# Splitting the last tile of a decoder trunk's output: 384 and 128 tokens in place of 256 and 256

## The chip, the cores and the metric

One core of a Trainium2 chip runs the whole program. The metric is the device time of one execution in microseconds; before the change it is 1289.63 us, the median of 3 runs (1287.84 to 1291.17).

## What is computed

A two-layer decoder trunk over 512 tokens of 1024 features in float32: a mixer (state-space and gated recurrence) and a gated ConvFFN, then dilated window attention and a second ConvFFN, and a final RMSNorm. The change touches only the very end, which the reference writes as

```python
    h = h + ff.astype(h.dtype)
return _rmsnorm(h, norm_final)
...
def _rmsnorm(x, g):
    xf = x.astype(jnp.float32)
    y = xf * lax.rsqrt(jnp.mean(xf * xf, axis=-1, keepdims=True) + NORM_EPS)
    return (y * g.astype(jnp.float32)).astype(x.dtype)
```

where `ff` is the down projection of the second ConvFFN: a product of 2816 by 1024 weights with the activations of 512 tokens.

## The kernel before

The activations are held transposed: a tile is 128 features (partitions) by 512 tokens (columns). The down projection in `ffn` (line 863) makes 8 such output tiles, `m` = 0 to 7, each a sum over `NF` = 22 blocks of the inner width. For full precision each block is three matmuls (`mm3`, lines 187 to 189): high weights by high activations, low weights by high activations, high weights by low activations, all in the reduced float32 format of TensorE (`F32R`), so 66 matmuls a tile. Each has weights of its own (128 by 128), which are loaded just ahead of it; its moving operand is the tokens.

In layer 1 the tiles `m` = 0 to 6 are made over all 512 tokens (lines 905 to 910), and as each is done, VectorE adds it to the residual `h` (line 909, tile H in the trace) and `norm_add` brings its squares into the sums `ss` and writes `hg`, which is h times the gain (tile xh in the trace; line 249 on ScalarE).

The last tile, `m` = 7, is made in two halves of 256 tokens (lines 914 to 926), so that the final norm of the first half's tokens runs beside the matmuls of the second half. For each half, in this order of dependence:

- 66 matmuls of 256 columns into a bank `pt`;
- line 921, VectorE: add to H;
- line 237, ScalarE: the square, into `sq`; line 249, ScalarE: `hg`;
- `rms_cols`, line 261, TensorE: small plain float32 matmuls with one column against a constant of 1/1024, first on `ss` (which is ready early), then on `sq`, so that the mean square of each token lands in a column of a bank `px`;
- lines 265, 207 and 210 to 212, VectorE: 11 tiny operations, the inverse root, into `rc`;
- `rms_rows`, line 273, TensorE: one transpose for each 128 tokens, which spreads `rc` over all partitions;
- line 925, VectorE: four products of two feature tiles each, `hg` times the inverse root, into `o` (tile xl in the trace);
- line 926: a DMA to the output after each product, by turns from the queues of SyncE (SP) and ScalarE (ACT).

Program order is not execution order: the framework's scheduler interleaves the instructions of one engine when the program is built, by its own estimates, and the order on each engine is then fixed. TensorE works strictly through that list of matmuls. So a small matmul of the first half's norm stands at a fixed place among the second half's matmuls, and TensorE waits there if its operand isn't ready.

Of the kernel before, what the change touches and what calls it, by code (L numbers as in the profile page):

```python
# [12 lines left out]
OP = mybir.AluOpType  # L13
# [3 lines left out]
KD = 8  # L17
# [138 lines left out]
class Kernel:  # L156
# [706 lines left out]
    def ffn(self, layer, gi):  # L863
        tc, nc, a, h = self.tc, self.nc, self.a, self.h
        V = nc.vector
        with tc.tile_pool(name="wkf", bufs=2) as self.wk, tc.tile_pool(name="ff1", bufs=1) as p1:
            self.nb = 5
            cw = p1.tile([128, 2 * NF, 4], F32, name="cw")
            nc.scalar.dma_start(cw, a["conv"][:, layer])
            ah = p1.tile([128, NF, T], F32R, name="ah")  # L870
            al = p1.tile([128, NF, T], F32R, name="al")
            hus = [p1.tile([128, T + 2], F32, name=f"hu{i}") for i in range(4)]
            for x in hus:
                nc.gpsimd.memset(x[:, 0:2], 0.0)
            w = Weights(self, a[f"w_f{layer}"], 1024)
            ahead = [self.proj(w) for _ in range(3)]
            rs = self.rms_rows(self.rms_cols())
            for j in range(NF):
                half = []
                for s in range(2):  # L880
                    f = 2 * j + s
                    x, pt, y = hus[f % 4], ahead.pop(0), self.tmp()
                    if f + 3 < 2 * NF:
                        ahead.append(self.proj(w))
                    V.tensor_tensor(x[:, 2:], pt, rs, op=OP.mult)  # L885
                    nc.scalar.activation(y, x[:, 2:], AF.Identity, scale=cw[:, f, 2:3], bias=cw[:, f, 3:4])  # L886
                    V.scalar_tensor_tensor(y, x[:, 1:T + 1], cw[:, f, 1:2], y, op0=OP.mult, op1=OP.add)  # L887
                    V.scalar_tensor_tensor(y, x[:, 0:T], cw[:, f, 0:1], y, op0=OP.mult, op1=OP.add)  # L888
                    half.append(y)
                nc.scalar.activation(half[0], half[0], AF.Silu)  # L890
                V.tensor_tensor(half[0], half[0], half[1], op=OP.mult)  # L891
                self.split(ah[:, j], al[:, j], half[0])
            w = Weights(self, a[f"w_g{layer}"], 1024)
            self.norm(gi, layer == 0)
            parts = []

            def block(m, q):
                n = m * NF + q
                if n // 8 == len(parts):
                    parts.append(w.next())  # L900
                hi, lo = parts[n // 8]
                b = slice(128 * (n % 8), 128 * (n % 8) + 128)
                return hi[:, b], lo[:, b]

            for m in range(KD if layer == 0 else KD - 1):
                pt = self.accbank()
                for q in range(NF):
                    self.mm3(pt, *block(m, q), ah[:, q], al[:, q], q == 0, q == NF - 1)
                V.tensor_tensor(h[:, m], h[:, m], pt, op=OP.add)  # L909
                self.norm_add(m, h[:, m])  # L910
            if layer == 0:
                return

            m = KD - 1
            o = self.xp.tile([128, KD, T], F32, name="xl")
            pts = [self.accbank() for _ in range(2)]
            for s in range(2):
                t = slice(256 * s, 256 * s + 256)
                for q in range(NF):
                    self.mm3(pts[s][:, t], *block(m, q), ah[:, q, t], al[:, q, t], q == 0, q == NF - 1)  # L920
                V.tensor_tensor(h[:, m, t], h[:, m, t], pts[s][:, t], op=OP.add)
                self.norm_add(m, h[:, m, t], t=t)
                rs = self.rms_rows(self.rms_cols(blocks=(2 * s, 2 * s + 1)), copy=False, blocks=(2 * s, 2 * s + 1))
                for i in range(0, KD, 2):
                    V.tensor_tensor(o[:, i:i + 2, t], self.hg[:, i:i + 2, t], rs[:, None, t].to_broadcast([128, 2, 256]), op=OP.mult)
                    (nc.scalar if i % 4 else nc.sync).dma_start(self.out[:, i:i + 2, t], o[:, i:i + 2, t])


    def attention(self):
# [335 lines left out]
```

## Time and profile before

| | |
|---|---|
| median of 3 runs | 1289.63 us (1287.84 to 1291.17) |
| the profiled execution's own time | 1289.94 us |
| its span, first to last instruction | 1288.1 us |
| TensorE busy | 1242.9 us, 96% of the span |
| VectorE busy | 812.5 us, 63% |
| ScalarE busy | 540.5 us, 42% |
| mean granted TensorE clock | 0.99 |

The span covers the instructions; the execution's own time is 1.84 us longer and holds what lies around them. Busy time is that of an engine's instructions, whether anything waits for them or not; what an engine is worth at a given place is read from the chain of waits and from the timeline there. In the timeline a row gives the start, the time taken, the engine and line, and the operands as out<-in; a matmul's time is that of one matmul from start to end, and since matmuls are pipelined, the step from one start to the next is the rate.

### The profile page before, as it was taken

How to read it: one execution, taken by the hardware profiler on the slowest of the kernel's cores; microseconds unless marked ns; L12 is line 12 of the kernel's file. 1: busy time of each engine (PE TensorE's matmuls, PEld its weight loads, DVE VectorE, ACT ScalarE, POOL GpSimd, SP SyncE). 2: the span in 40 equal slices, each digit the busy share in tenths (PEclk: the TensorE clock that was granted, in tenths of full speed). 3: DMA queues.
4: the chain of work that ended last, by engine and by line, in shares of the span. 5: the costliest groups of instructions: out<-in, count | busy, mean ns of one | idle time of the engine just before them, and what ended most of it. 6: DMA issues, size and time to landing. Idle time of an engine off the chain costs nothing.

```text
span 1288.1 us, 18925 instructions
## 1 busy us (share of the span) xinstructions
PE 1242.9 (96%) x7826; PEld 1019.4 (79%) x7826; DVE 812.5 (63%) x1342; ACT 540.5 (42%) x827; POOL 109.7 (9%) x87
## 2 busy tenths in 40 slices
PE   8889997999999999999999999999899999999997
PEld 6667775878888888888788887897688888888886
DVE  8786877958777776333563536556787777773223
ACT  6447646435444444222334333434354444442221
POOL 1443000110000000000120102100300000000000
PEclk9999998999999999999999999999999999999999
DMA  6532431232222222222322332322222222222211
GB/s 212 156 111 65 131 99 51 99 101 98 95 92 92 94 94 95 95 98 98 116 80 98 95 99 74 108 85 68 68 99 98 98 98 98 98 98 98 99 66 66
DMA packets 41126, 125.14 MB, mean 97 GB/s; under 512 B 18320, under 2 KB 22480, under 8 KB 28368
## 3 DMA queue, kind: packets, MB, share of 16 engines
q1 hardware_dynamic: 27744, 115.16, 27.2%
q10 hardware_dynamic: 13296, 8.78, 2.4%
q8 instruction: 61, 1.00, 0.3%
q14 instruction: 25, 0.20, 0.0%
HBM read 117.57 MB, written 4.78 MB: 95 GB/s over the span
## 4 chain that ended last, share of the span: by engine, by line
PE 83%; DVE 10%; DMA 2%; ACT 2%; issue 1%; POOL 1%; SPq 0%; DVEq 0%; ACTq 0%; POOLq 0%
PE pt L187 26%; PE pt L189 25%; PE pt L188 25%; DVE wlo L127 2%; PE px L1095 1%; DVE xl L231 1%; PE px L1120 1%; POOL g L765 1%; DMA b<-yd 1%; PE px L1179 1%; POOL g L758 1%; PE px L1092 0%; PE px L187 0%; PE px L847 0%; PE px L189 0%
## 5 line engine op out<-in xcount | busy, mean ns | idle before, releaser
L187 PE MATMUL pt<-xh,whi 128*128 128x512 f32 x1008 | 398.6, 396 | 4.0 <-ACT whi L126 2.3
L127 DVE TENSOR_TENSOR wlo<-stg,whi 128x1024 fp32r<-128x1024 f32 (+1 forms) x205 | 253.0, 1235 | 232.0 <-ACT whi L126 229.4
L189 PE MATMUL pt<-xl,whi 128*128 128x512 f32 x1008 | 393.8, 391 | 1.9 <-DVE xl L231 1.3
L188 PE MATMUL pt<-xh,wlo 128*128 128x512 f32 x1008 | 394.3, 391 | 0.3 <-DVE wlo L127 0.3
L126 ACT ACTIVATE whi<-stg 128x1024 fp32r<-128x1024 f32 (+1 forms) x205 | 214.3, 1046 | 264.4 <-PE pt L189 219.1
L187 PEld LDWEIGHTS pt<-xh,whi 128*128 128x128 f32 x1008 | 190.3, 189 | 46.3 <-issue 2.6
L189 PEld LDWEIGHTS pt<-xl,whi 128*128 128x128 f32 x1008 | 189.4, 188 | 43.1 <-DVE xl L231 2.4
L188 PEld LDWEIGHTS pt<-xh,wlo 128*128 128x128 f32 x1008 | 190.3, 189 | 39.8 <-DVE wlo L127 0.7
L187 PE MATMUL pt<-ah,whi 128*128 128x512 f32 (+1 forms) x374 | 142.4, 381 | 0.0
L189 PE MATMUL pt<-al,whi 128*128 128x512 f32 (+1 forms) x374 | 141.8, 379 | 0.0
L188 PE MATMUL pt<-ah,wlo 128*128 128x512 f32 (+1 forms) x374 | 140.4, 376 | 0.0
L885 DVE TENSOR_TENSOR hu<-pt,rs 128x512 f32<-128x512 f32 x88 | 60.2, 688 | 62.9 <-PE pt L189 60.0
L189 PEld LDWEIGHTS pt<-al,whi 128*128 128x128 f32 x374 | 70.2, 188 | 14.5
L188 PEld LDWEIGHTS pt<-ah,wlo 128*128 128x128 f32 x374 | 70.2, 188 | 13.9
L187 PEld LDWEIGHTS pt<-ah,whi 128*128 128x128 f32 x374 | 70.3, 188 | 12.4
L886 ACT ACTIVATE b<-hu,cw 128x512 f32<-128x512 f32 x88 | 70.7, 807 | 5.1 <-DVE hu L885 4.4
L193 ACT ACTIVATE ah<-b 128x512 fp32r<-128x512 f32 x44 | 27.7, 630 | 107.3 <-DVE b L891 107.3
L888 DVE SCALAR_TENSOR_TENSOR b<-hu,cw,b 128x512 f32<-128x512 f32 x88 | 65.9, 751 | 2.8
L887 DVE SCALAR_TENSOR_TENSOR b<-hu,cw,b 128x512 f32<-128x512 f32 x88 | 65.5, 746 | 0.0
L890 ACT ACTIVATE b<-b 128x512 f32<-128x512 f32 x44 | 27.8, 632 | 72.9 <-DVE b L888 72.9
L239 POOL TENSOR_TENSOR ss<-H 128x512 f32<-128x512 f32 x4 | 4.2, 1042 | 608.1 <-DVE H L909 506.7
L187 PE MATMUL pt<-whi,xh 128*128 128x512 f32 x128 | 53.5, 418 | 0.0
(308 smaller groups left out, 1438.4 us busy)
## 6 DMA issues: line engine op xcount, KB each, us to landing
stg<-w_f SPq DMA_DIRECT2D x44, 1024.0 KB
stg<-w_g SPq DMA_DIRECT2D x22, 1024.0 KB
stg<-w_qkv SPq DMA_DIRECT2D x18, 1024.0 KB
stg<-w_mix SPq DMA_DIRECT2D x8, 1024.0 KB
stg<-w_mo SPq DMA_DIRECT2D x4, 1024.0 KB
H<-xT SPq DMA_DIRECT2D x8, 256.0 KB
b<-xT ACTq DMA_DIRECT2D x8, 256.0 KB
wrow<-wd SPq DMA_DIRECT2D x8, 256.0 KB
```

The source lines that it names most:

```text
L126: nc.scalar.activation(hi[:, c], s[:, c], AF.Copy)
L127: nc.vector.tensor_tensor(lo[:, c], s[:, c], hi[:, c].bitcast(F32), op=OP.subtract)
L187: mm(pt, sh, mh, start=first, stop=False)
L188: mm(pt, sl, mh, start=False, stop=False)
L189: mm(pt, sh, ml, start=False, stop=last)
L193: nc.scalar.activation(hi, x, AF.Copy)
L231: nc.vector.scalar_tensor_tensor(self.xl[:, i], x, g, self.xh[:, i].bitcast(F32), op0=OP.mult, op1=OP.subtract)
L885: V.tensor_tensor(x[:, 2:], pt, rs, op=OP.mult)
L886: nc.scalar.activation(y, x[:, 2:], AF.Identity, scale=cw[:, f, 2:3], bias=cw[:, f, 3:4])
L887: V.scalar_tensor_tensor(y, x[:, 1:T + 1], cw[:, f, 1:2], y, op0=OP.mult, op1=OP.add)
L888: V.scalar_tensor_tensor(y, x[:, 0:T], cw[:, f, 0:1], y, op0=OP.mult, op1=OP.add)
L890: nc.scalar.activation(half[0], half[0], AF.Silu)
```

## The change

The last tile's two parts become blocks 0, 1, 2 (384 tokens) and block 3 (128 tokens). In the second part the products of line 925 take four feature tiles at a time in place of two, so that there are two of them and two DMAs.

```diff
-            for s in range(2):
-                t = slice(256 * s, 256 * s + 256)
+            for s, (blocks, n) in enumerate((((0, 1, 2), 2), ((3,), 4))):
+                t = slice(128 * blocks[0], 128 * blocks[-1] + 128)
                 for q in range(NF):
                     self.mm3(pts[s][:, t], *block(m, q), ah[:, q, t], al[:, q, t], q == 0, q == NF - 1)
                 V.tensor_tensor(h[:, m, t], h[:, m, t], pts[s][:, t], op=OP.add)
                 self.norm_add(m, h[:, m, t], t=t)
-                rs = self.rms_rows(self.rms_cols(blocks=(2 * s, 2 * s + 1)), copy=False, blocks=(2 * s, 2 * s + 1))
-                for i in range(0, KD, 2):
-                    V.tensor_tensor(o[:, i:i + 2, t], self.hg[:, i:i + 2, t], rs[:, None, t].to_broadcast([128, 2, 256]), op=OP.mult)
-                    (nc.scalar if i % 4 else nc.sync).dma_start(self.out[:, i:i + 2, t], o[:, i:i + 2, t])
+                rs = self.rms_rows(self.rms_cols(blocks=blocks), copy=False, blocks=blocks)
+                for i in range(0, KD, n):
+                    V.tensor_tensor(o[:, i:i + n, t], self.hg[:, i:i + n, t], rs[:, None, t].to_broadcast([128, n, 128 * len(blocks)]), op=OP.mult)
+                    (nc.scalar if i // n % 2 else nc.sync).dma_start(self.out[:, i:i + n, t], o[:, i:i + n, t])
```

On TensorE the change moves the small matmuls of the first part's norm to other places among the second part's matmuls. From the matmuls on `ss` to those on `sq` (both line 261; the last matmul of the first part stands just ahead of them), before:

```order
L261 MATMUL px<-cst,ss_9419 32x1 x8
L187 MATMUL pt<-ah,whi 128x256
L188 MATMUL pt<-ah,wlo 128x256
L189 MATMUL pt<-al,whi 128x256
L187 MATMUL pt<-ah,whi 128x256
L188 MATMUL pt<-ah,wlo 128x256
L189 MATMUL pt<-al,whi 128x256
L187 MATMUL pt<-ah,whi 128x256
L188 MATMUL pt<-ah,wlo 128x256
L261 MATMUL px<-cst,sq_10102 32x1 x8
```

and now:

```order
L261 MATMUL px<-cst,ss_9419 32x1 x12
L187 MATMUL pt<-ah,whi 128x128
L188 MATMUL pt<-ah,wlo 128x128
L189 MATMUL pt<-al,whi 128x128
L187 MATMUL pt<-ah,whi 128x128
L188 MATMUL pt<-ah,wlo 128x128
L261 MATMUL px<-cst,sq_10102 32x1 x12
```

So 8 of the second part's matmuls stood between the two and now 5 do, and each of the two has 12 small matmuls in place of 8. The second place is around the transposes of line 273, which wait for VectorE's `rc`; here with the tiles' numbers, of which 10006, 10045 and 10073 are the high weights of the tile's first 6, next 8 and last 8 blocks. Before:

```order
L188 MATMUL pt_10024<-ah_7741,wlo_10046 128x256
L189 MATMUL pt_10024<-al_7742,whi_10045 128x256
L187 MATMUL pt_10024<-ah_7741,whi_10045 128x256
L273 MATMUL px_10137<-cst_73,rc_10122 128x128 x2
L188 MATMUL pt_10024<-ah_7741,wlo_10046 128x256
L189 MATMUL pt_10024<-al_7742,whi_10045 128x256
```

and now:

```order
L189 MATMUL pt_10024<-al_7742,whi_10006 128x128
L187 MATMUL pt_10024<-ah_7741,whi_10006 128x128
L188 MATMUL pt_10024<-ah_7741,wlo_10007 128x128
L273 MATMUL px_10145<-cst_73,rc_10130 128x128 x3
L189 MATMUL pt_10024<-al_7742,whi_10006 128x128
L187 MATMUL pt_10024<-ah_7741,whi_10006 128x128
```

The transposes came in the ninth block and now come in the fifth: 17 matmuls stood between the `sq` matmuls and them, and now 9 do; 41 of the second part's 66 came behind them, and now 52 do.

On ScalarE the difference is this piece, from the last full tile's `hg` to the end of the program:

```order
 L249 ACTIVATE xh<-H,gn 128x512
-L237 ACTIVATE sq_10102<-H 128x256
-L249 ACTIVATE xh<-H,gn 128x256
-L926 DMA out<-xl 128x2x256 x2
-L237 ACTIVATE sq_10102<-H 128x256
-L249 ACTIVATE xh<-H,gn 128x256
-L926 DMA out<-xl 128x2x256 x2
+L237 ACTIVATE sq_10102<-H 128x384
+L249 ACTIVATE xh<-H,gn 128x384
+L926 DMA out<-xl 128x2x384 x2
+L237 ACTIVATE sq_10102<-H 128x128
+L249 ACTIVATE xh<-H,gn 128x128
```

Behind the last row stands one DMA of 128x4x128 in place of two. Nothing changes its place on ScalarE; the sizes do, and the second square still stands behind the first part's two DMAs. SP likewise issues two DMAs for the first part and one for the second in place of two, and VectorE two products in place of four at the end.

## Rows read from the trace of the kernel before

**Rows 1.** The page's head: the span.
```profile
span 1288.1 us, 18925 instructions
```

**Rows 2.** Busy time by stretch: us, PE, PEld, DVE, ACT, POOL, PEclk, DMA share, GB/s.
```profile
1268.69:1277.82 9.13, 9.08 (x101) 8.58 (x100) 4.68 (x16) 0.82 (x2) 0.00 (x0) 1.00 0.35 116
1277.82:1282.01 4.19, 1.08 (x35) 0.63 (x34) 2.20 (x13) 0.81 (x2) 0.00 (x0) 0.96 0.01 2
1282.01:1284.50 2.49, 0.00 (x0) 0.00 (x0) 2.48 (x4) 0.00 (x0) 0.00 (x0) 0.50 0.36 119
```

**Rows 3.** Timeline of TensorE: matmuls of the last full tile and the first half.
```profile
1254.42 0.39 PE L189 MATMUL pt<-al,whi 128*128 128x512 f32 x1
...
1260.60 0.39 PE L189 MATMUL pt<-al,whi 128*128 128x512 f32 x1
1260.83 0.28 PE L187 MATMUL pt<-ah,whi 128*128 128x256 f32 x1
...
1268.48 0.28 PE L189 MATMUL pt<-al,whi 128*128 128x256 f32 x1
```

**Rows 4.** Timeline during the second half: the first half's norm, and the last matmul.
```profile
1270.07 0.31 PE L261 MATMUL px<-cst,sq 128*32 128x1 f32 x16
...
1270.45 0.16 DVE L265 TENSOR_SCALAR ms<-px 128x2 f32<-128x2 f32 x1 [1.23 <-PE px L261]
...
1272.41 0.16 DVE L212 SCALAR_TENSOR_TENSOR rc<-rqt,rc 128x2 f32<-128x2 f32 x1
1272.63 0.43 PE L273 MATMUL px<-cst,rc 128*128 128x128 f32 x2
...
1273.02 0.28 PE L189 MATMUL pt<-al,whi 128*128 128x256 f32 x1
...
1273.10 2.48 DVE L925 TENSOR_TENSOR xl<-xh,px 128x512 f32<-128x512 f32 x4 [0.53 <-PE px L273]
...
1277.62 0.28 PE L189 MATMUL pt<-al,whi 128*128 128x256 f32 x1
```

**Rows 5.** The chain that ended last, behind the last matmul: start us, us, what.
```profile
1277.93 0.43 DVE H L921
...
1278.39 0.42 ACT sq L237
...
1278.86 0.35 PE px L261 x16
...
1281.50 0.48 PE px L273 x2
...
1282.01 0.69 DVE xl L925
```

**Rows 6.** Groups by line and shape: add and square of 512 columns (mean ns).
```profile
L909 DVE TENSOR_TENSOR H<-H,pt 128x512 f32<-128x512 f32 x15 | 10.3, 686 | 17.9 <-PE pt L189 17.9
L237 ACT ACTIVATE sq<-H 128x512 f32<-128x512 f32 x17 | 10.5, 618 | 3.9 <-DVE H L909 2.4 <-DVE ss L241 1.6
```

**Rows 7.** Plain float32 matmuls of 128 columns: timeline of layer 0, and their group.
```profile
123.77 0.60 PE L586 MATMUL px<-v,attd 128*128 128x128 f32 x4
...
126.00 1.04 PE L780 MATMUL px<-cst,g 128*128 128x128 f32 x8
```
```profile
L586 PE MATMUL px<-v,attd 128*128 128x128 f32 x32 | 5.5, 274 | 0.0
```

**Rows 8.** Weight loads by shape: 128 and 64 columns (busy us, mean ns).
```profile
L187 PEld LDWEIGHTS pt<-ah,whi 128*128 128x128 f32 x374 | 70.3, 188 | 12.4
...
L554 PEld LDWEIGHTS px<-hb 128*64 128x64 f32 x32 | 2.2, 138 | 2.5 <-DVE hb L570 1.8 <-issue 0.4 <-DVE hb L529 0.4
```

**Rows 9.** Output DMAs of the second half: issue, transfer; and packets of 512 bytes elsewhere.
```profile
1282.72 1.57 SPq L926 DMA_DIRECT2D out<-xl  x2
```
```profile
1283.40:1287.00 3.60, 0.00 (x0) 0.00 (x0) 1.09 (x2) 0.00 (x0) 0.00 (x0) 0.50 0.88 291
```
```profile
DMA packets 189, 0.09 MB, mean 269 GB/s; under 512 B 5, under 2 KB 189, under 8 KB 189
```

## The prediction

> **What bounds the kernel now.** The page's span [rows 1] is nearly all matmul stream, but the change lies in its last 28 us, so I read the stretches there first, then TensorE's timeline, and then the chain of waits behind the last matmul. TensorE is busy in 9.08 of the 9.13 us of the second half's stretch [rows 2], and the chain goes from its last matmul, which starts at 1277.62 [rows 4], through VectorE's add, ScalarE's square, the small matmuls, the transposes and the products [rows 5] to the output DMAs. Two things thus set the end: how long the second part's matmuls run, and how long the tail behind them is. The change shortens the tail and cannot take a column off the stream: 384 + 128 is 256 + 256.
>
> From the rates to see in the timeline [rows 3]: 27 steps from 1254.42 to 1260.60 give 0.2289 us a matmul of 512 columns; 65 steps from 1260.83 to 1268.48 give 0.1177 us at 256. The difference is 0.1112 us for 256 columns, so 384 columns should take 0.1733 us. This lies between two measured sizes and is safe. For 128 columns the trace has no matmul of this format at all, and on that price the forecast turns.
>
> **The price at 128 columns.** Carrying the line of the two sizes on gives 0.0621 us, the low end. But every matmul has 128 columns of weights of its own to load. A load of 64 columns is 138 ns and one of 128 is 188 ns [rows 8], 0.78 ns a column, so 128 columns keep the load path for 0.10 us if loads don't overlap each other. At 256 columns that is hidden under the columns themselves; at 128 it is not. The nearest rows with this tile shape are layer 0's plain float32 matmuls of 128 columns with 128 columns of weights: from 123.77 to 126.00 there are 20 of them (4, 2, 2, 4, 2 and 6 in a row), 0.1115 us each [rows 7]. They read their columns differently, so they don't prove the load bound, but they show that loads can follow each other at that pace, and they agree with the 0.10. I take **0.1115 us**: barely less than at 256 columns. The high end is 0.2289 us, if 128 columns cost what 512 do now; the rows for it are under the first rival.
>
> The Trainium skill (TensorE: Matmul & The Clock Gate, section Back-to-back issue gap) gives about 81 ns a matmul as the sustained rate of load and matmul pairs at 128 columns, less than rows 7 show; by it the sum below would be 50 x 0.0305 = 1.5 us lower, an estimate from that page. No row here goes as low for a full load, so I don't take it.
>
> **The stream, step by step.** The first part starts where it did, 1260.83, and its last matmul starts at 1260.83 + 65 x 0.1733 = 1272.09. The first part's norm then follows the pattern of the second half's tail:
> - Matmul start to add: 0.31 us (1277.62 to 1277.93), and 0.05 more for a longer matmul: 1272.46.
> - Add to square: 0.46 us at 256 columns; 512 columns take 0.686 in place of 0.43 [rows 6], so 384 add 0.13: 1273.05.
> - Square to the `sq` matmuls: 0.47 us; 618 ns in place of 0.42 at 512 columns, so 384 add 0.10: 1273.62.
> - `sq` matmuls to the mean: 0.38 us (1270.07 to 1270.45), and half of 0.35 us again for half as many more: 1274.17.
> - Mean to transposes: 2.18 us (1270.45 to 1272.63 [rows 4]), whatever the number of columns, 2 or 3: 1276.35.
>
> In the new order only nine matmuls stand between the `sq` matmuls and the transposes. At 0.1115 they take 1.0 us, and the norm takes 2.7. So **a new wait** opens: TensorE stands still for about 1.2 us ahead of the transposes, with the other 52 matmuls queued behind. Before, 17 matmuls of 0.1177 filled nearly that time. From the transposes to the second matmul behind them it was 0.39 us (1272.63 to 1273.02); one more transpose adds 0.11 (the eight of line 780 take 1.04 us [rows 7]): 1276.85. The last matmul starts 50 steps later: 1276.85 + 50 x 0.1115 = 1282.43, against 1277.62: **+4.8 us**.
>
> **The tail.** With 128 columns in place of 256 the last matmul ends 0.05 us sooner; the add saves 0.13 and the square 0.10 (the same slopes as above); half of the small matmuls go, 0.17 of 0.35; one transpose of two goes, 0.11. Together -0.56. The 11 tiny operations between keep their time: they have two elements a partition or one. So the first product starts at 1282.01 + 4.8 - 0.56 = 1286.26.
>
> From its start the old tail took 4.99 us until the last data had left (1282.01 to 1287.00): the first DMA is issued at 1282.72, data flow from about 0.8 us later, and the queue is full from then on, 1.05 MB at 291 GB/s over 3.6 us [rows 9]. Now the first product is as long as before (512 elements), data flow from 1.5 us after its start, and half of the bytes remain. They go in runs of 512 bytes in place of 1024; the trace has a stretch of such packets at 269 GB/s, so 0.52 MB take 1.95 us: 3.45 in place of 4.99, **-1.5 us**. If a packet of 512 took the time of one of 1024 nothing would be won there; if the rate held at 291, another 0.15. The second of the two products ends at 1.3 us and its DMA's data can flow from 2.1 us, within that time.
>
> Costed at nothing: the first part's products, 4 of 768 elements in place of 512, take 2.48 x 1.5 = 3.7 us [rows 4] and end near 1280.7, before the second part's add at 1282.7; and ScalarE, whose second square stands behind two DMAs that wait for these products, is free by then. The work that hides both is the second part's stream; it is cover only while that stream lasts.
>
> **Sum:** 4.8 - 0.56 - 1.5 = +2.7 us. The profiled execution took 1289.94 us, its span 1288.1; it lies 0.3 above the median of the three runs. 1289.63 + 2.7 = **1292.3 us**, 0.21% more. About 0.3%, 3.9 us, is what a measurement of this kernel can tell from no change, so I call this the same.
>
> **Rivals.**
>
> *First, a matmul of 128 columns is far dearer than one of 256.* Line 586 is called 16 times in the program (four heads, four blocks) and has 32 records [rows 7]: a plain float32 product of 128 columns takes two passes of 0.1115, so 0.22 us, what 512 columns of the reduced format cost. If TensorE handles the reduced format like plain float32 in short matmuls, or streams it in one quarter of the speed, the price is 0.22 to 0.2289. Against it: from 512 to 256 columns nothing but a fixed 0.0065 us stays [rows 3]. The transposes would come at nearly the same time, since five and nine matmuls then take 1.15 and 2.1 us, about what the norm takes. The end moves by 50 x (0.2289 - 0.1115) = 5.9, 0.17 for a longer last matmul and some 0.1 of shift: 2.7 + 6.1 = +8.8, **1298.4 us**, slower. It decides from 0.135 us a matmul on, where 2.7 + 50 x 0.0235 passes 3.9. The Trainium skill (FP8 and Floating Point Precision, section TensorE Precision Notes) keeps four passes for true float32 and has the reduced format read and cut down, without a word on length; that speaks against the rival, and no row here shows it at 128 columns.
>
> *Second, columns alone count.* At 0.0621 the stream ends 2.5 us sooner, but the first part's products then hold VectorE until 1280.7, where the add would be due at 1280.2: +2.7 - 2.5 + 0.4 = +0.6, **1290.2 us**. For it: the straight line from 512 to 256. Against it: rows 7 and 8. Even so there is no gain, as the new wait eats it.
>
> *Third, the granted clock falls in the new wait.* It is 1.00 through the second half, 0.96 over the 4.2 us behind it, which hold few matmuls, and 0.50 after that [rows 2]. At 0.50, the lower of its two levels, 1.2 in place of 2.4 GHz, the 52 matmuls would take 0.22 us each and the time would be near that of the first rival, 1298. Against it: the wait is 1.2 us, and in the tail the clock held for some 3.5 us behind the last big matmul.
>
> **How the numbers follow.** Forecast 0.55, first rival 0.34, second 0.06, third 0.03, and 0.02 for a gain that I don't see. The forecast's own range is 1290.8 (price 0.10, cheap data) to 1294.0 (price 0.1177, dear packets, the scatter of the runs); a tenth of it lies above 3.9 us and counts as slower. Faster by over 0.3%: 0.02. Within: 0.5 and the second rival, 0.55. Slower: 0.34, 0.03 and 0.06, so 0.43. Cases of two kinds hold the chance, so the range takes both: 1289.9 to 1299.4.
>
> **What would show it.** Steps of 0.173 us in the first part; a step of 0.11 in the second (0.06 or 0.22 for the rivals); TensorE waiting about 1.2 us for `rc` ahead of the transposes of line 273 (none if the price is 0.22); the last matmul near 1282.4; 4.5 us from the first product of the last tail to the end of the span, against 6.1. If the granted clock drops between 1274 and 1282, the third rival is right. If the end of the stream lies before 1280, my price is wrong on the low side.

## The result, and the profile after

The change makes the kernel slower. Its median is 1296.33 us (1295.50 to 1298.94, 6 runs) against 1290.00 (1287.84 to 1291.17, 6 runs of the kernel before, the three known ahead of the prediction among them); the ratio is 1.0055, with a 95% interval of 1.0042 to 1.0069, so +7.1 us (5.4 to 8.9). The time lies in the predicted range, but not where the likeliest case put it: 1292.3, no difference that can be measured. What happened is the third rival, which had 0.03. That the range holds the time is luck: it reached that far for the first rival's price, which the rows below exclude.

The page's head of the kernel after answers to [rows 1]; the execution that was profiled took 1295.50 us, with a mean granted clock of 0.984 against 0.99:

```profile
span 1293.7 us, 18920 instructions
```

Spans of two executions can't simply be subtracted here: the last tile's first part starts at 1260.83 in [rows 3] and at 1257.71 now, and over all the profiles of this study at 1257.15 to 1260.83, with nothing changed in the code ahead of it. So I count from that start, called S below. From S to the end of the span it was 27.27 us before, and it is 35.99 now: +8.7.

Windows by stage of the kernel after, with the columns of [rows 2] (stretch and its length, then busy time of PE, PEld, DVE, ACT and POOL, PEclk, DMA share, GB/s). The stretches are the first part's matmuls; from there to the last matmul ahead of the new wait; the wait, cut in two where the clock fell; the matmuls behind it; the tail; the output:

```profile
1257.71:1269.10 11.39, 11.39 (x67) 11.28 (x65) 2.52 (x3) 0.96 (x2) 2.33 (x2) 1.00 0.00 0
...
1269.31:1272.10 2.79, 2.52 (x63) 2.21 (x62) 1.47 (x7) 1.03 (x2) 0.00 (x0) 1.00 0.02 6
1272.10:1272.54 0.44, 0.00 (x0) 0.00 (x0) 0.37 (x3) 0.00 (x0) 0.00 (x0) 1.00 0.00 0
1272.54:1273.20 0.66, 0.00 (x0) 0.00 (x1) 0.50 (x4) 0.00 (x0) 0.00 (x0) 0.50 0.00 0
...
1273.20:1284.67 11.47, 11.47 (x54) 11.47 (x55) 3.55 (x4) 0.00 (x0) 0.00 (x0) 0.50 0.38 137
1284.67:1288.89 4.22, 1.37 (x19) 0.81 (x19) 2.04 (x12) 0.60 (x2) 0.00 (x0) 0.50 0.00 0
1288.89:1293.70 4.81, 0.00 (x0) 0.00 (x0) 1.28 (x2) 0.00 (x0) 0.00 (x0) 0.50 0.39 109
```

Read the PEclk column downwards. It is 1.00 (2.4 GHz) until 0.44 us into the wait, then 0.50 (1.2 GHz), and it never comes back, although TensorE is busy in all 11.47 us of the stretch behind. In [rows 2] the second half ran at 1.00 from start to end.

The timeline of the kernel after, answering to [rows 3, 4] (in the gaps the pattern repeats):

```profile
1268.97 0.34 PE L189 MATMUL pt<-al,whi 128*128 128x384 f32 x1
...
1269.35 0.56 DVE L921 TENSOR_TENSOR H<-H,pt 128x384 f32<-128x384 f32 x1 [6.27 <-PE pt L189]
...
1270.57 0.37 PE L261 MATMUL px<-cst,sq 128*32 128x1 f32 x24 [0.26 <-ACT sq L237]
...
1271.04 0.28 PE L187 MATMUL pt<-ah,whi 128*128 128x128 f32 x1
...
1271.82 0.28 PE L188 MATMUL pt<-ah,wlo 128*128 128x128 f32 x1
...
1272.98 0.16 DVE L212 SCALAR_TENSOR_TENSOR rc<-rqt,rc 128x3 f32<-128x3 f32 x1
...
1273.20 0.90 PE L273 MATMUL px<-cst,rc 128*128 128x128 f32 x3 [1.11 <-DVE rc L212]
...
1274.22 0.41 PE L188 MATMUL pt<-ah,wlo 128*128 128x128 f32 x1
...
1284.67 0.41 PE L189 MATMUL pt<-al,whi 128*128 128x128 f32 x1
```

The 384-column step is (1268.97 - 1257.71) / 65 = 0.1732 us. The 128-column step ahead of the wait is (1271.82 - 1271.04) / 7 = 0.111. Then TensorE stands still for 1.11 us, for `rc`. Behind it the same matmuls step by (1284.67 - 1274.22) / 49 = 0.2133 us: from 0.111 to 0.213, nearly twice, with the clock at half.

The chain that ended last, behind the last matmul, answering to [rows 5]:

```profile
1285.12 0.30 DVE H L921
1285.44 0.32 ACT sq L237
1285.81 0.33 PE px L261 x8
1288.41 0.46 PE px L273
1288.89 0.69 DVE xl L925
```

From the last matmul to the first product it is 4.22 us (4.39 before), and from there to the end of the span 4.81 (6.09 before). The sum of the changes: the last matmul at S + 26.96 against S + 16.79, +10.17; -0.17 and -1.28 behind it; +8.7.

### The profile page after: what moved, and what is told of

Same layout as the page of the kernel before. It is cut to its first block, busy times and chain, and to the rows that moved or that the text cites. A ratio compares the mean times of both kernels' runs of the same rounds, so it can differ in the third digit from the quotient of the medians.

```text
span 1293.7 us, 18920 instructions
## 1 busy us (share of the span) xinstructions
PE 1249.8 (97%) x7826; PEld 1026.5 (79%) x7826; DVE 814.1 (63%) x1340; ACT 540.5 (42%) x827; POOL 109.7 (8%) x87
## 4 chain that ended last, share of the span: by engine, by line
PE 83%; DVE 10%; DMA 2%; issue 2%; ACT 1%; POOL 1%; DVEq 0%; ACTq 0%; SPq 0%; POOLq 0%
PE pt L187 26%; PE pt L189 26%; PE pt L188 25%; DVE wlo L127 2%; PE px L1095 1%; DVE xl L231 1%; PE px L1120 1%; PE px L1179 1%; POOL g L765 1%; POOL g L758 1%; PE px L1092 0%; DVE hb L570 0%; DVE ss L241 0%; PE px L847 0%; PE px L546 0%
## 5 line engine op out<-in xcount | busy, mean ns | idle before, releaser
L187 PE MATMUL pt<-ah,whi 128*128 128x512 f32 (+2 forms) x374 | 146.0, 390 | 0.0
L189 PE MATMUL pt<-al,whi 128*128 128x512 f32 (+2 forms) x374 | 145.4, 389 | 0.0
L188 PE MATMUL pt<-ah,wlo 128*128 128x512 f32 (+2 forms) x374 | 143.9, 385 | 0.0
L189 PEld LDWEIGHTS pt<-al,whi 128*128 128x128 f32 x374 | 72.9, 195 | 14.5
```

The lines of the kernel that those rows point to most:

```text
L187: mm(pt, sh, mh, start=first, stop=False)
L188: mm(pt, sl, mh, start=False, stop=False)
L189: mm(pt, sh, ml, start=False, stop=last)
```

## The experiments

Two theories stood at the start, and the third came up after the first four runs. **A**: the standstill ahead of the transposes lets the clock fall. **B**: the matmuls of 128 columns ("narrow" below, those of 256 "wide"), which the prediction takes to go at the pace of their weight loads, make it fall by themselves. **C**: the narrow matmuls ahead of the wait have a share in it too. For all but one of the experiments the last tile was written so that its order on TensorE can be set: `k1` and `k2` are the numbers of the second part's matmuls ahead of the small `sq` matmuls (the sums) and ahead of the transposes, 5 and 14 in the change, `cols` the columns that the second part's matmuls run over. Where `force` is set, each piece is tied behind the small matmuls on TensorE's list:

```diff
-            for s, (blocks, n) in enumerate((((0, 1, 2), 2), ((3,), 4))):
...
+            first, second, cols, k1, k2, force = ((0, 1, 2), 2), ((3,), 4), slice(384, 512), 5, 14, True
...
+            late(0, k1)
+            rc = self.rms_cols(blocks=first[0])
+            with after(self.last):
+                late(k1, k2)
+            rs = self.rms_rows(rc, copy=False, blocks=first[0])
+            with after(self.last):
+                late(k2, 3 * NF)
```

The diffs below are against this form. Where `cols` is wider than 128 columns, the columns outside block 3 go to a part of the bank that nothing reads. Every ratio below is against runs of the kernel before on the same chip. The experiments were spread over three chips, so where two of them are compared it is by these ratios or by their spans from S, which are those of one profile each.

**No wait.** The sums and transposes come so late that neither waits.

```diff
-            first, second, cols, k1, k2, force = ((0, 1, 2), 2), ((3,), 4), slice(384, 512), 5, 14, True
+            first, second, cols, k1, k2, force = ((0, 1, 2), 2), ((3,), 4), slice(384, 512), 17, 46, False
```

> Parts of 384 and 128 tokens as in the change, but the first part's sums stand behind 17 of the second part's matmuls and its transposes behind 46, so that nothing makes TensorE wait inside the second part. Theory A (the 1.3 us wait ahead of the transposes drops the granted clock, and it stays down because nothing raises it again): no wait, so the clock stays 1.00 through the second part, all its steps are 0.111 us, and the kernel is about 1.2 us over the kernel before (+3.2 us of matmuls, -2.0 us of tail). Theory B (the load-paced matmuls of 128 columns drop the clock by themselves): the clock falls to 0.50 about 3 us into the second part although there is no wait, the steps behind that are 0.21 us, and the kernel is 4.5 to 6.5 us over.

Measured: 1291.23 us (1287.97 to 1293.72, 10 runs), ratio 1.0023 (1.0009 to 1.0038). The second part's matmuls, in the windows of this kernel:

```profile
1270.67:1278.90 8.23, 8.23 (x124) 8.07 (x123) 4.48 (x15) 1.03 (x2) 0.00 (x0) 1.00 0.04 12
```

The clock holds over all 66 narrow matmuls; the last one starts at S + 19.59, not 26.96. That speaks for A and against B. But the transposes are late now, and the cover that the prediction named for the first part's products is gone. From the timeline of VectorE (here line 934 is the products, line 949 the second part's add):

```profile
1276.75 3.55 DVE L934 TENSOR_TENSOR xl<-xh,px 128x768 f32<-128x768 f32 x4 [1.58 <-PE px L273]
1280.22 0.28 DVE L949 TENSOR_TENSOR H<-H,pt 128x128 f32<-128x128 f32 x1
```

The add could have started 0.32 us behind the last matmul of 1278.62, at 1278.94, and waits 1.28 us for the products. Theory A had the whole at 1.2 us over the kernel before, without this wait; from S to the end it is 2.7 us over.

**The old halves, with the change's wait.** Parts of 256 and 256, sums behind 5 and transposes behind 14.

```diff
-            first, second, cols, k1, k2, force = ((0, 1, 2), 2), ((3,), 4), slice(384, 512), 5, 14, True
+            first, second, cols, k1, k2, force = ((0, 1), 2), ((2, 3), 2), slice(256, 512), 5, 14, True
```

> Halves of 256 and 256 as before the change, but with the wait of the change: the first half's sums behind 5 and its transposes behind 14 of the second half's matmuls, and the other 52 held behind them. Theory A: the clock falls in the wait of about 1.2 us as it does with the change, and the 52 matmuls of 256 columns then take 0.21 us or more for as long as it stays down: 5 to 7 us over the kernel before. Theory B: the clock stays 1.00, the steps stay 0.118 us, and only the waits are paid: about 1.5 us over.

Measured: 1289.92 us (one run). The clock falls, from the timeline's steps just behind the wait, and it comes back:

```profile
1269.62:1273.36 3.74, 3.74 (x19) 3.74 (x20) 2.48 (x4) 0.00 (x0) 0.00 (x0) 0.54 0.45 146
1273.36:1277.70 4.34, 4.34 (x42) 4.20 (x44) 0.00 (x0) 0.00 (x0) 0.00 (x0) 1.00 0.34 116
```

So a wait among matmuls of 256 columns can cost the clock too, but there it is back after some 3.4 us. Neither theory had that: from S the end is 2.7 us later than before, where A had 5 to 7 us, with the clock down for longer, and B about 1.5, without a fall.

**The change's wait with 256 columns behind and ahead.** The second part's matmuls run over 256 columns, and half of that is thrown away.

```diff
-            first, second, cols, k1, k2, force = ((0, 1, 2), 2), ((3,), 4), slice(384, 512), 5, 14, True
+            first, second, cols, k1, k2, force = ((0, 1, 2), 2), ((3,), 4), slice(256, 512), 5, 14, True
```

> The change with its wait (sums behind 5, transposes behind 14 matmuls of the second part), but the second part's matmuls run over the last 256 tokens, of which the first 128 are thrown away: the same number of matmuls and loads, twice the columns. Theory A: the clock falls in the wait as with the change; the steps behind it are 0.21 us or more, and the kernel is 7 us or more over the kernel before. Theory B: the clock stays 1.00 and the steps 0.118 us, twice the columns are faster than half of them, and the kernel is about 3 us over (+3.6 first part, +1.5 waits, -2.0 tail).

Measured: 1290.58 us (one run), with the clock at 1.00 through the wait and behind it:

```profile
1272.66:1273.76 1.10, 0.10 (x2) 0.00 (x1) 0.87 (x6) 0.00 (x0) 0.00 (x0) 1.00 0.00 0
1273.76:1280.20 6.44, 6.44 (x62) 6.31 (x63) 3.55 (x4) 0.00 (x0) 0.00 (x0) 1.00 0.63 224
```

Twice the columns, and from S to the end 30.53 us where the change takes 35.99: the columns are not what the change pays for. By itself this run came out as B expected (clock 1.00, about 3 us over; from S 3.3 us); it is the first sign that the standstill alone doesn't settle the matter: as long a wait, and no fall.

**The narrow part first.** Block 0, then blocks 1 to 3.

```diff
-            for s, (blocks, n) in enumerate((((0, 1, 2), 2), ((3,), 4))):
+            for s, (blocks, n) in enumerate((((0,), 4), ((1, 2, 3), 2))):
```

> The 128 tokens first and the 384 second: 66 matmuls of 128 columns follow the 512-column stream with nothing between them. Theory A: clock 1.00 and 0.111 us a step throughout, 7.3 us for the first part; the kernel is about 5.5 us over the kernel before, for the longer tail of 384 tokens. Theory B: the clock falls to 0.50 some 3 us into the first part, the rest of it runs at 0.21 us a step, so the part takes 10 us or more; whether the 384-column matmuls behind it raise the clock again shows what keeps it down.

Measured: 1293.35 us (one run). The 66 narrow matmuls run in 7.4 us at full clock:

```profile
1259.03:1266.40 7.37, 7.37 (x67) 7.33 (x65) 2.51 (x3) 0.96 (x2) 2.31 (x2) 1.00 0.00 0
```

With the first experiment this ends theory B: where no standstill stood among them or ahead of them, the narrow matmuls ran at full clock to the last. From S the end is 5.2 us later than before (A had about 5.5): 3.0 of it at the last matmul, and 2.2 behind it, where the tail now has 384 tokens.

**The wait filled.** The change's order, and five matmuls of 512 columns between the 14th matmul and the transposes, whose result is not used.

```diff
-                late(k1, k2)
+                self.mid = late(k1, k2)
+            with after(self.mid):
+                fb = self.auxbank()
+                for i in range(5):
+                    hi, lo = block(m, 0)
+                    self.fil = nc.tensor.matmul(fb, hi, ah[:, 0], start=True, stop=True)
+            with after(self.fil):
                 rs = self.rms_rows(rc, copy=False, blocks=first[0])
```

> The change with its order (sums behind 5, transposes behind 14 matmuls of the second part), but five matmuls of 512 columns into a bank that nobody reads fill the wait ahead of the transposes. Theory A (the standstill drops the clock): the clock stays 1.00 through the second part, steps of 0.111 us, and the kernel is 2.5 to 3 us over the kernel before, what the sum without a clock change gave. Theory B (the light matmuls drop it, or the light matmuls and small sums around the wait): the clock falls as with the change, 52 steps of 0.21 us, 6 to 8 us over.

Measured: 1292.81 us (1291.65 to 1293.71, 5 runs), ratio 1.0037 (1.0024 to 1.0050). The wait's stretch, and the matmuls behind it:

```profile
1274.77:1276.14 1.37, 1.37 (x8) 0.84 (x7) 1.02 (x7) 0.00 (x0) 0.00 (x0) 1.00 0.00 0
1276.14:1282.40 6.26, 6.26 (x61) 6.19 (x63) 3.55 (x4) 0.00 (x0) 0.00 (x0) 1.00 0.62 222
```

TensorE does work that nothing needs, the transposes come 0.1 us later than with the change (S + 15.59), and the last matmul starts 5.4 us sooner, at S + 21.58. That is +4.79 against before, where the prediction had +4.8 for a clock that holds. Theory A had 2.5 to 3 us over for the whole; from S to the end it is 3.2, while the ratio makes it 4.8 (3.1 to 6.5).

**Wide ahead of the wait, narrow behind.** Here `cols` is set for each of the second part's matmuls, by its number `i`.

```diff
+                    cols = slice(256 if i < 14 else 384, 512)
```

> The same order and the wait left empty; the second part's first 14 matmuls run over 256 columns (128 thrown away), the 52 behind the wait over 128. Theory A in the form that the standstill alone decides: the clock falls in most runs and stays down for the 52, so 6 to 8 us over the kernel before. Theory C (the 14 light matmuls ahead of the wait count too, since the same wait behind wide ones kept its clock in one look and lost it for 3.4 us in another): in a good part of the runs the clock holds and they are about 3 us over, in the others it falls, and with 128 columns it doesn't come back.

Measured: 1290.81 us (1289.33 to 1297.50, 10 runs), ratio 1.0026 (1.0012 to 1.0040). Eight of the ten lie at 1289.3 to 1293.0 and two at 1295.4 and 1297.5; the profile is of one of the two. The wait, and the stretches to the fall and behind it:

```profile
1274.15:1275.15 1.00, 0.00 (x1) 0.00 (x0) 0.81 (x5) 0.00 (x0) 0.00 (x0) 1.00 0.00 0
1275.15:1277.42 2.27, 2.27 (x21) 2.27 (x21) 1.69 (x2) 0.00 (x0) 0.00 (x0) 1.00 0.00 0
1277.42:1285.40 7.98, 7.80 (x45) 7.59 (x43) 2.15 (x4) 0.04 (x1) 0.00 (x0) 0.50 0.55 197
```

The clock falls not in the wait but 2.3 us behind it, in the middle of narrow matmuls that follow each other without a gap, and then stays down. By their times eight of the ten runs are of the kind that C had (about 3 us over, which is also the median) and not of A's (6 to 8 us over in most).

**Narrow ahead, wide behind.**

```diff
+                    cols = slice(256 if i == 0 or i >= 14 else 384, 512)
```

> The mirror image: 13 of the first 14 matmuls over 128 columns, then the empty wait, then 52 matmuls over 256 columns (128 thrown away). The clock should fall in the wait as with the change in all theories but one that blames the light matmuls behind it; what is tested is the way back: if full columns raise it as in the halves with a wait (back after 3.4 us), about 14 of the 52 run at 0.23 us and the rest at 0.118, so the kernel is 4 to 5 us over the kernel before, faster than the change though it streams twice the columns; if the clock stays down to the end as with the change, it is 8 us over or more.

Measured: 1293.12 us (1290.41 to 1295.70, 7 runs), ratio 1.0034 (1.0019 to 1.0049), in two groups, three runs at 1290.4 to 1291.6 and four at 1293.1 to 1295.7. The profile, of the first group, shows no fall, neither in the 1.1 us of the wait nor behind it, where a fall in the wait had been expected:

```profile
1273.67:1274.77 1.10, 0.00 (x1) 0.01 (x1) 0.87 (x6) 0.00 (x0) 0.00 (x0) 1.00 0.00 0
1274.77:1281.40 6.63, 6.63 (x59) 6.50 (x61) 3.55 (x4) 0.00 (x0) 0.00 (x0) 1.00 0.64 228
```

**No wait, with the transposes earlier.** As the first experiment, but early enough that VectorE's products are less in the way.

```diff
-            first, second, cols, k1, k2, force = ((0, 1, 2), 2), ((3,), 4), slice(384, 512), 5, 14, True
+            first, second, cols, k1, k2, force = ((0, 1, 2), 2), ((3,), 4), slice(384, 512), 14, 40, False
```

> As the run without a wait (384 and 128), but with the sums behind 14 and the transposes behind 40 matmuls of the second part in place of 17 and 46, so that the first part's products hold VectorE less beyond the stream's end. Theory A: clock 1.00, 0.111 us a step, 1.2 us for the late add of that run falls to 0.5 us or less: 1.5 to 2 us over the kernel before, within 0.3%. Theory B: the clock falls and the kernel is 4.5 us over or more.

Measured: 1290.40 us (1289.22 to 1292.88, 12 runs), ratio 1.0022 (1.0013 to 1.0032): this is the best form of 384 and 128 found, and still slower than before. The second part's window, its last matmul and the add:

```profile
1270.79:1279.20 8.41, 8.41 (x123) 8.25 (x125) 5.14 (x16) 1.03 (x2) 0.00 (x0) 1.00 0.11 40
...
1278.94 0.28 PE L925 MATMUL pt<-al,whi 128*128 128x128 f32 x1
1279.87 0.28 DVE L949 TENSOR_TENSOR H<-H,pt 128x128 f32<-128x128 f32 x1
```

The clock is 1.00 over the second part; the add still comes 0.61 us late (0.5 or less was expected), at S + 20.52 behind a last matmul of S + 19.59. That matmul itself is 2.8 us later than before; from S to the end it is 2.0 us over, as A had it.

**The control.** The form above with nothing changed: the change's order, and an empty wait.

> The control for the run with the filled wait: the same code, 128 columns in the second part, sums behind 5 of its matmuls and transposes behind 14, and nothing in the wait. Theory A (the standstill ahead of the transposes drops the granted clock): the clock goes to 0.50 inside the wait and stays there, the 52 matmuls behind it step by 0.2135 us, and the time lies where the change's lies, 6 to 8 us over the kernel before and at least 3 over the filled wait. Theory B (the load-paced matmuls of 128 columns drop it themselves): the same fall, which then should have come in the filled wait too. If instead this run holds 1.00 and lies 3 to 5 us over, the difference between the change and the filled wait was the layout of the code or the chip, and theory A loses its main support.

Measured: 1296.94 us (1294.39 to 1297.46, 4 runs), ratio 1.0054 (1.0036 to 1.0072). The wait up to the fall, the rest of it, and the matmuls behind:

```profile
1274.02:1274.44 0.42, 0.00 (x1) 0.00 (x0) 0.35 (x3) 0.00 (x0) 0.00 (x0) 0.99 0.00 0
1274.44:1275.13 0.69, 0.00 (x0) 0.00 (x0) 0.53 (x4) 0.00 (x0) 0.00 (x0) 0.50 0.00 0
...
1275.13:1286.90 11.77, 11.77 (x55) 11.70 (x55) 3.54 (x4) 0.00 (x0) 0.00 (x0) 0.50 0.37 134
```

It is the change again: the fall 0.42 us into the wait, the last matmul at S + 26.96, the end at S + 35.96 (35.99 with the change). The filled wait ends at S + 30.45, so in these two profiles filling 1.1 us of standstill is worth 5.5 us. By the ratios it is less (1.0054 against 1.0037, some 2 us), and their intervals overlap. The filled runs were on another chip than the control; the run without a wait, which kept its clock too and ended at S + 29.97, was on the control's; its ratio is 1.0023 (1.0009 to 1.0038).

**Narrow ahead and wide behind, again.** The kernel of that name above once more, for a second profile.

> The kernel with 13 of the first 14 matmuls of 128 columns, the empty wait, and 52 of 256 behind it, once more, for a profile of its slower kind: its times stood in two groups, 1290.4 to 1291.6 and 1293.1 to 1295.7, and the profile fell in the first. Theory A with a way back: where the clock falls in the wait, the 256-column matmuls raise it again within some 4 us (3.4 us in the run with 256 on both sides), and the fall costs about 15 matmuls by 0.1 us, 1.7 us. Theory that a fall stays down until the end whatever follows: 52 matmuls of 0.22, the time near 1296. No fall in this profile would leave it open.

Measured: 1291.44 us (one run), and no fall in the wait or behind it:

```profile
1273.34:1274.44 1.10, 0.00 (x1) 0.01 (x1) 0.87 (x6) 0.00 (x0) 0.00 (x0) 1.00 0.00 0
1274.44:1281.10 6.66, 6.66 (x61) 6.53 (x63) 3.55 (x4) 0.00 (x0) 0.00 (x0) 1.00 0.64 230
```

Without a fall the run says nothing of the way back.

**Wide ahead and narrow behind, again.**

> The kernel with 256 columns ahead of the empty wait and 128 behind it, once more, for a profile of its usual kind: its time was 1289.3 to 1293.0 in most runs, and the profile fell in one of the two at 1295 to 1298. If the usual kind is one with no fall: the clock is 1.00 through the second part, the last matmul starts 21.6 to 21.9 us after the first part's start, 52 steps of 0.111, and about 1290.6 us; the wait then lets the clock fall only where light matmuls lie around it on either side. If the clock falls in this one as well, at the wait or behind it, the time should be near 1295.

Measured: 1298.10 us (one run), so it is not of the kind that most runs were of: the clock holds through the wait and is down over the 52 narrow matmuls behind it.

```profile
1274.84:1275.85 1.01, 0.00 (x1) 0.00 (x1) 0.81 (x5) 0.00 (x0) 0.00 (x0) 1.00 0.00 0
1275.85:1287.60 11.75, 11.75 (x55) 11.68 (x55) 3.55 (x4) 0.00 (x0) 0.00 (x0) 0.50 0.38 134
```

So wide matmuls ahead of the wait are no protection, and theory C is at most a matter of how often: two of ten runs by their times, and this one.

**Narrow ahead and for 20 matmuls behind, then wide.** The last question was whether a fall at this place can be undone.

```diff
+                    cols = slice(256 if i == 0 or i >= 34 else 384, 512)
```

> The change's order with its empty wait, all but the first of the first 34 matmuls over 128 columns (13 ahead of the wait, 20 behind it), and the last 32 over 256, where the control had 128 to the end. With no fall the last matmul starts some 21.8 us after the first part's start, and the time is 1291 to 1292. Theory A (the fall comes in the wait; narrow matmuls keep it down, wide ones raise it again): the clock goes to 0.50 in or shortly behind the wait, stays there for the 20 narrow matmuls, which cost 20 x 0.10 = 2.0 us, and comes back to 1.00 within some 4 us of wide ones, another 1.5: the last matmul near 25.3, the time near 1295. Theory D (a fall at this place stays to the end whatever follows): all 52 step by 0.21 to 0.235, the last matmul near 27 to 27.4, the time 1297. The profile tells the two apart if the clock falls in it; if it doesn't, the way back stays shown by the one run with a wait between halves.

Measured: 1294.42 us (1289.37 to 1296.61, 8 runs), ratio 1.0046 (1.0028 to 1.0064). The wait up to the fall and from there, the transposes with the 20 narrow matmuls, and the wide ones up to the clock's return and from there:

```profile
1271.54:1272.38 0.84, 0.00 (x0) 0.00 (x0) 0.70 (x5) 0.00 (x0) 0.00 (x0) 1.00 0.00 0
1272.38:1272.64 0.26, 0.00 (x1) 0.00 (x1) 0.17 (x2) 0.00 (x0) 0.00 (x0) 0.50 0.00 0
```

```profile
1272.64:1277.50 4.86, 4.86 (x24) 4.86 (x24) 3.55 (x4) 0.00 (x0) 0.00 (x0) 0.50 0.42 151
1277.50:1282.51 5.01, 5.01 (x24) 5.01 (x25) 0.00 (x0) 0.00 (x0) 0.00 (x0) 0.50 0.47 168
1282.51:1283.79 1.28, 1.28 (x18) 1.15 (x17) 0.00 (x0) 0.00 (x0) 0.00 (x0) 0.96 0.00 0
```

The clock comes back, 5.0 us behind the first wide matmul. That is later than the 4 us that I had given theory A, and the last matmul, at S + 26.36, lies between the two expectations; but the return itself is what theory D denied. Up to the wait this kernel and the one with 52 wide matmuls behind have the same instructions on TensorE. That one held the clock in both profiles of its wait, this one lost it: what stands on TensorE's list doesn't decide alone whether a given execution falls. (The three profiles are of three chips; that a chip has a share in it isn't excluded.)

## Why the prediction was right and wrong

**The prices were right.** 384 columns: 0.1733 predicted, 0.1732 measured. 128 columns: 0.1115 taken, 0.111 measured, at full clock. So going from 256 to 128 columns saves 0.007 us of 0.118. That the weight loads set this pace, as the prediction argued, fits the price but isn't shown: no run has narrow matmuls that share their weights. The 81 ns that the Trainium skill gives (TensorE: Matmul & The Clock Gate, section Back-to-back issue gap) were not reached: over the 66 narrow matmuls at full clock the step is 0.111 us (7.21 / 65 with the narrow part first), and the measurement decides.

**The norm and the wait were right.** From S, add 11.63 predicted and 11.64 measured, sums 12.79 and 12.86, transposes 15.52 and 15.49. The wait is 1.1 us where 1.2 stood, with another 0.26 ahead of the sums.

**The stream was right for a clock that holds.** With the wait filled the last matmul comes 4.79 us later than before; predicted, 4.8. With the change it comes 10.17 later. The difference is 5.38: 52 steps of 0.2133 in place of 0.111 make 5.3, and the slower transposes about the rest.

**The tail was a little too good.** -0.56 to the first product: -0.36 with the filled wait, -0.17 at the low clock, where the small matmuls and the transpose are slower. -1.5 for the output: -1.25 and -1.28. Without the fall the whole stretch comes to +3.2 (filled wait), where the sum said +2.7.

**The step that failed** is the third rival's chance, and with it the likeliest case, which kept the clock at 1.00 behind the new wait. It rests on this sentence: "Against it: the wait is 1.2 us, and in the tail the clock held for some 3.5 us behind the last big matmul." I took one row of [rows 2], the tail behind 256-column matmuls, as a hold time that any standstill has to outlast. In the change's profile the clock held for 0.44 us of the wait. And the price that the rival gave, 52 matmuls of 0.22, assumed that the clock would stay down for all of them; I gave no reason for that, and it is the half that the experiments made clear. A fall is followed by a return where the matmuls behind are of 256 columns (3.4 and 5.0 us), and by none where they are of 128 (8 to 11.8 us in four profiles, to the end of the stream each time). Of the cause of this the profiles say no more. With a way back after 3.4 us, some 16 matmuls would have cost 0.10 us more each: by this estimate 1.6 us in place of 5.3. The rival's place and its time, 1298, were right to within 2 us; its 8.8 us is the 8.7 from S. The measured 7.1 is less, but its interval reaches to 8.9.

**The first rival gave the same time** (1298.4) for another reason, and the time alone could not have told the two apart: 0.2133 us a matmul behind the wait is what it predicted. The nine narrow matmuls ahead of the wait at 0.111, and the same matmuls at 0.111 everywhere in the filled wait, exclude it.

**The second rival** is excluded by the same rows. What it said of VectorE showed elsewhere: where the transposes were moved back to avoid the wait, the products held up the second part's add by 1.28 and 0.61 us. The cover lasted as long as the stream, as the prediction had it.

**What stays open.** What in an execution decides whether the clock falls. With the change's order and an empty wait both profiles show the fall; that the other eight of the ten runs fell is read from their times (1294.39 us or more, where no run of the kernel before in this study took over 1292.45). Their mean clock of 0.981 to 0.986 is a weak sign, since single runs of the kernel before have 0.985 and 0.986. In the four profiles with no wait or a filled one the clock doesn't fall before the stream's end. Of the nine with an empty wait six show the fall, 0.42 to 3.27 us behind the wait's start, and three show none, all three with wide matmuls behind the wait. Three of the five with narrow matmuls ahead of the wait lost the clock in the wait and two held it. That the wait brings the change's fall is shown, since taking it away in two ways (moving the transposes, filling the gap) kept the clock; that a wait always brings one is not so, and the exact condition stays open.

No order of 384 and 128 that was run beats the halves. The best, the second one without a wait, stands at a ratio of 1.0022 (1.0013 to 1.0032), some +2.8 us: 66 matmuls at 0.111 bring a quarter of the columns, and no order that was run makes up for that.

## What to carry to other kernels

A short standstill of TensorE can cost more than its length when the matmuls behind it are narrow: here 1.1 us cost another 5.4 in the profiles, because the clock fell and didn't come back among 128-column matmuls in any of four profiles. So when an edit makes matmuls narrower, look where they meet a wait, and either move the waiting instruction back in the queue, as far as its own readers allow, or fill the gap. And before cutting a stream unevenly, divide its time by its matmuls: a part whose step hardly falls with its columns (here 0.118 us at 256 and 0.111 at 128) only gets shorter in columns, not in time.

## What the runs showed of the hardware

- At 0.50 a matmul of this format with weights of its own takes the same for 128 and for 256 columns: 0.2133 us with the change, and (1277.50 - 1273.44) / 19 = 0.2137 narrow against (1282.30 - 1277.82) / 21 = 0.2133 wide in the last experiment. A matmul of 128 columns thus is 0.111 or 0.213 us, and one of 256 is 0.118 or 0.213.
- 66 narrow matmuls ran at 1.00 for 7.4 us behind a stream without a gap. Behind a wait the clock fell in the middle of such matmuls in one profile, 2.3 us behind the wait's end. Where it was at 0.50, it was still there after 52 of them in 11.5 us, with PE busy by the profile throughout; with wide matmuls it was back at 1.00 after 3.4 us in one profile and 5.0 us in another.
- Two profiles of one kernel held the clock through the wait, and one of another, with the same instructions on TensorE up to there, lost it 0.84 us in.
